# A hybrid decoder block on one core: both products of a bank ahead of their Squares in the linear attention, and one sum of the down projection queued behind the low part next to it

## The chip, the core and the metric

The kernel runs on one core of a Trainium2 chip. The metric is the device time of one execution in microseconds (us); the smaller the better. Five engines run side by side, each with its own in-order queue: TensorE (PE; its weight loads are shown apart as PEld), VectorE (DVE), ScalarE (ACT), GpSimd (POOL) and SyncE (SP, which issues most transfers here). They wait for one another through semaphores.

## The reference, cut to what matters

One decoder layer over 512 tokens of width 1024, in float32. A projection gives the inputs of two token mixers: a gated linear attention (4 heads, keys of 128, values of 256) and a sparse attention. Their outputs are merged, projected and added to the input; a SwiGLU channel mixer of width 2816 follows.

```
b = cumsum(log_a)                       # per head, in chunks of 64 tokens
qe, ke, kd = q*exp(b), k*exp(-b), k*exp(b_last - b)
o = causal(qe @ ke.T) @ v               # inside a chunk
o = o + qe @ s_prev                     # the state carried from the chunks before
o = o * rsqrt(mean(o*o) + eps) * norm_g # per token and head, over 256 values
...
f = (silu(h @ w_ffn_gate) * (h @ w_ffn_up)) @ w_ffn_down
x = x + rms_norm(f, norm_ffn_post)
```

The two places of the change are the line `o = ...` of the linear attention with the sum of squares of its norm, and the product with `w_ffn_down`.

## The kernel before, in words

**Products.** Float32 products are made in three passes: an operand is split into a high part (a cast, usually on ACT) and a low part (source minus high part, on DVE), and `three` (lines 266 to 276) issues high x high, high x low and low x high, seen in the trace as lines L269, L274 and L275. L274 loads the high part of the weight once more, and L275 loads its low part. `split` (L301 the cast, L303 the low part) makes the two parts. In a few products the low parts are left out and float32 operands go in as they are; such a matmul shows as two entries.

`restart()` makes the next 256-column product issue its second pass as two passes of 128 columns. It is called at chosen places; one is in the loop over the eight plain row blocks of the down projection.

**Linear attention.** Each head goes through `gla_prep`, `gla_attn`, `gla_state`, `gla_out` and `gla_end`; these steps are woven between the products of the input projection (`eproduct`, made in seven half-size products of a Strassen-like form). `gla_out(h)` is where the change is. It has four blocks of 128 tokens. Two PSUM banks (`ps`, tag `acc`) hold two blocks each, 256 columns per block. For a block n it issues the product of the masked scores with the values (L806), for n > 0 a second product of the query with the carried state (L808), and then an ACT `Square` of that block (L809) with the sum over the row in `ssq`. Heads 0 and 1 use plain float32 products; heads 2 and 3 use `three`, so that their products stand under L269, L274 and L275. When the four sums are there, `rsqrt_mean` makes the factor (L317 on DVE, L318 on POOL), ACT scales the four blocks (L817), and `gla_end` transposes them (L832).

**Down projection.** The first 8 row blocks of the weight are done plainly (`sd`). The rest is four units u of the same seven-product form. The list `seq` gives the order of the 28 products: for u = 0 and 1 in turn a11, s2, s3, s1, a22, s4, a12, so that u = 1 has the places j = 7 to 13, and s3, s1, a22, s4 of it are j = 9, 10, 11, 12. `make(j)` prepares the weight of product j: `dsum` makes its sum on DVE where there is one, `split` makes the high and low parts (`lows[j]` is the DVE instruction of the low part), and for some j `dload` starts a transfer of the next unit's quarter. `make(j + 3)` is called after product j. The sum s4 (L1915) is r12 minus s2; the quarter r12 of unit 1 lands in the second half of the buffer `c_two`, by a transfer that `make(6)` starts.

**What sets the order.** Tiles are allocated by name, and the program's planner orders the instructions of each engine by when it estimates their inputs to be ready, with program order as the priority; the waits between engines follow from the data. A PSUM bank is guarded as a whole: a product into one half of a bank waits for a read of the other half. `tc.issue_after(x)` fixes an order by hand: what is issued inside stands behind `x` in the queue of x's engine, without a wait for x to end. `dsum` takes such an `after`, which before the change is used for the sum s2 alone.

Of the kernel before, what the change touches and what calls it, by code (L numbers as in the profile page):

```python
# [11 lines left out]
AF = mybir.ActivationFunctionType  # L12
OP = mybir.AluOpType
# [161 lines left out]
def hybrid_block_kernel(ctx: ExitStack, tc: tile.TileContext, I, outT):  # L175
    nc = tc.nc
    act, dve, pool, pe = nc.scalar, nc.vector, nc.gpsimd, nc.tensor
# [13 lines left out]
    def bank(tag):  # L191
        return psum.tile([128, 512], F32, tag=tag, bufs=2, name="ps_" + tag)
# [47 lines left out]
    for key in with_gla + with_cmp + with_att + late:  # L240
        kind, n = key
# [23 lines left out]
    def three(o, w, x, start, stop):  # L265

        (wh, wl), (xh, xl) = w, x
        n = o.shape[1]
        pe.matmul(o, wh, xh, start=start, stop=False, skip_group_check=True)  # L269
        cut = [slice(0, 128), slice(128, 256)] if fresh[0] and n == 256 else [slice(0, n)]  # L270
        if n == 256:
            fresh[0] = False
        for c in cut:
            pe.matmul(o[:, c], wh, xl[:, c], start=False, stop=False, skip_group_check=True)  # L274
        stk["pe"] = pe.matmul(o, wl, xh, start=False, stop=stop, skip_group_check=True)  # L275
        return stk["pe"]
# [23 lines left out]
    def split(hi, lo, src, after=None):  # L300
        act.copy(hi, src)  # L301
        with tc.issue_after(after.ins) if after else nullcontext():
            return dve.tensor_tensor(out=lo, in0=src, in1=hi.bitcast(F32), op=OP.subtract)  # L303

    def token_sums(acc, tag, blocks=range(NT)):

        ps = bank(tag)
        for a in range(len(acc)):
            for i in blocks:
                stk["sums"] = pe.matmul(ps[:, i:i + 1], acc[a][:, i * 128:(i + 1) * 128], ones[:, 0:1],  # L310
                                        start=(a == 0 and i == blocks[0]), stop=(a == len(acc) - 1),
                                        skip_group_check=True)
        return ps

    def rsqrt_mean(out, ps, n, eps):
        with tc.high_priority():
            dve.tensor_scalar(out=out, in0=ps, scalar1=1.0 / n, scalar2=eps, op0=OP.mult, op1=OP.add)  # L317
            return pool.tensor_tensor(out=out, in0=out, in1=mhalf[:, 0:out.shape[1]], op=OP.pow)  # L318

    def over_partitions(rs, tag, blocks=range(NT), after=None):  # L320
        ps = bank(tag)
        with tc.issue_after(after.ins) if after else nullcontext():
            for i in blocks:
                stk["over"] = pe.transpose(ps[:, i * 128:(i + 1) * 128], rs[:, i:i + 1].to_broadcast([128, 128]),
                                           ident)
        return ps
# [260 lines left out]
    for g in range(3):  # L587
        pss = [bank(t) for t in tags[g]]
        for c in range(4):
# [6 lines left out]
            for i, kk, m in turns:  # L596
                if (g, c, i, kk, m) == (0, 3, 2, 0, 0):
                    ps = token_sums([acc_x], "acc")
# [4 lines left out]
                o = pss[i][:, 0:TW[g]]  # L603
                x, y = ((hu, wh), (hul, wh), (hu, wl))[m]
# [3 lines left out]
        if g == 0:  # L608
            ps = over_partitions(rs_x, "acc")
# [36 lines left out]
    lows = []  # L646
# [145 lines left out]
    def gla_out(h, after=None):  # L792
        q3, qk, ku, dec, kut, ss = gst[h]
        at = ats[h % 2]
        ps = [bank("acc"), bank("acc")]
        ssq = gt.tile([128, NT], F32, tag="gssq", bufs=2, name="gssq")
        o = gt.tile([128, NT, 256], F32, tag="go", bufs=1, name="go")
        for n in range(NT):
            out = ps[n // 2][:, (n % 2) * 256:(n % 2) * 256 + 256]
            if h >= 2:  # L800
                with tc.issue_after(after.ins) if after else nullcontext():
                    three(out, two_of[h, "a"][n], two_of[h, "v", n], True, n == 0)
                    if n > 0:
                        three(out, two_of[h, "q"][n], two_of[h, "s"][n - 1], False, True)
            else:
                pe.matmul(out, at[:, n, :], tok[n][:, h * 256:(h + 1) * 256], start=True, stop=(n == 0))  # L806
                if n > 0:
                    pe.matmul(out, q3[:, n].rearrange("p s t -> p (s t)"), ss[:, n - 1, :], start=False, stop=True)  # L808
            act.activation(out=o[:, n, :], in_=out, func=AF.Square, accum_out=ssq[:, n:n + 1])  # L809
        rs = gt.tile([128, NT], F32, tag="grs", bufs=2, name="grs")  # L810
        rsqrt_mean(rs, ssq, 256, EPS)

        def scaled(after=None):
            for n in range(NT):
                out = ps[n // 2][:, (n % 2) * 256:(n % 2) * 256 + 256]
                with tc.issue_after(after.ins) if after else nullcontext():
                    act.activation(out=o[:, n, :], in_=out, func=AF.Copy, scale=rs[:, n:n + 1])  # L817

        if h < 2:
            rest[h] = scaled  # L820
        else:
            scaled()
        gst[h] = o
# [97 lines left out]
    for h in range(2):  # L921
        steps.append(lambda h=h: gla_state(h))
        steps.append(lambda h=h: gla_out(h))
        steps.append(lambda h=h: [gla_attn(h + 1), rest.pop(h)(stk["cast"])])
        steps.append(lambda h=h: gla_prep(h + 2))
        steps.append(lambda h=h: gla_end(h))
# [429 lines left out]
    for n in range(8):  # L1356
        ps = bank("sc")
# [41 lines left out]
    def w_slot(which):  # L1399

        if which == "w":
            return (wts.tile([128, 1024], F32R, tag="whi", bufs=2, name="whi"),
                    wts.tile([128, 1024], F32R, tag="wlo", bufs=2, name="wlo"))
        if which in ("d0", "d1", "c"):
            t = double(which)
            return t[:, 0:1024], t[:, 1024:2048]
        tags = {"u": ("uu", "uu"), "g3": ("g3h", "g3l"), "rw": ("rw", "rw")}[which]
        return tuple(wtile(t) for t in tags)
# [20 lines left out]
    for n in range(3):  # L1429
        ps = bank("mm")  # L1430
# [454 lines left out]
    draw, dw, loaded, lows = {}, {}, {}, {}  # L1885
    two_raw = double("c", F32)

    def dload(u, q):
        if u >= 4:
            return  # L1890
        if u == 3:
            raw = flat(quad("hh%d" % ("12", "22", "21", "11").index(q), F32, "raw" + q))
        elif q == "12":
            raw = two_raw[:, 1024:2048]
        else:
            raw = wts.tile([128, 1024], F32, tag="wraw", bufs=3, name="wraw")
        r, c = int(q[0]) - 1, int(q[1]) - 1
        with tc.issue_after(loaded[1, "22"].ins) if u == 3 else nullcontext():
            loaded[u, q] = nc.sync.dma_start(raw[:, :KW], I["w_down"][2 * u + r, :, c * KW:(c + 1) * KW])
        draw[u, q] = raw[:, :KW]  # L1900

    def dsum(u, name, after=None):
        r11, r12, r21, r22 = [draw[u, q] for q in ("11", "12", "21", "22")]
        if name == "s2":
            dve.tensor_tensor(out=r21, in0=r11, in1=r21, op=OP.subtract)
            x = two_raw[:, :KW]
            with tc.issue_after(after.ins) if after else nullcontext():
                dve.tensor_tensor(out=x, in0=r22, in1=r21, op=OP.subtract)
            draw[u, "s3"], draw[u, "s2"] = r21, x
        elif name == "s1":  # L1910
            dve.tensor_tensor(out=r11, in0=r11, in1=draw[u, "s2"], op=OP.add)
            draw[u, "s1"] = r11
        elif name == "s4":
            x = draw[u, "s2"]
            dve.tensor_tensor(out=x, in0=r12, in1=x, op=OP.subtract)  # L1915
            draw[u, "s4"] = x


# [6 lines left out]
    ends = {}  # L1925

    def make(j):
        if j >= len(seq):
            return
        u, a, b = seq[j]  # L1930
        behind = ends.get(j - 5) or ends.get(j - 7) if a == "s2" else None
        with tc.issue_after(behind.ins) if behind else nullcontext():
            dsum(u, a, (None, lows.get(7), None, ends.get(j - 3))[u])
        hi, lo = [x[:, :KW] for x in w_slot(("w", "g3", "w")[j % 3])]
        lows[j] = split(hi, lo, draw[u, a if a[0] == "s" else a[1:]])
        dw[u, a] = (hi, lo)
        if a in after_form and u < 2:
            dload(u + 1, after_form[a])
# [3 lines left out]
    for n in range(8):  # L1942
        ps = bank(("mm", "sc", "acc", "tp")[n % 2 + n // 4 * 2])
# [13 lines left out]
        if n == 6:  # L1957
            for q in ("21", "11", "22", "12"):
                dload(0, q)
            make(0)  # L1960
            make(1)
    make(2)

    def last_forms(i):
# [141 lines left out]
    ps = bank("tp")  # L2106
# [32 lines left out]
    for k in range(4):  # L2139
        for i in range(2):  # L2140
            c, x = i * 128, byrow[:, i, k * 128:(k + 1) * 128]
# [4 lines left out]
    for k in range(2):  # L2146
        dve.scalar_tensor_tensor(out=y2[k][:, t], in0=back[:, k * 256:k * 256 + 256], scalar=g_fpost[:, k:k + 1],
                                 in1=x1s[k][:, t], op0=OP.mult, op1=OP.add)
# [87 lines left out]
```

## Time and profile before

| | |
|---|---|
| median of 3 runs | 829.97 us (829.06, 829.97, 830.84) |
| the profiled execution's own time | 828.92 us |
| its span, first to last instruction | 826.7 us |
| mean granted TensorE clock | 0.999 |
| PE busy | 817.1 us, 99% |
| PEld, DVE, ACT, POOL busy | 751.2, 638.8, 533.7, 138.8 us |

How to read it: the span is what the trace covers, and the profiled execution took 2.2 us more than that around it. Busy time counts a matmul from its start to its modelled end, so matmuls that overlap in the pipeline leave PE busy without a gap; how fast PE runs is read from the starts of its matmuls and from how many of them stand in a stretch. Times in the rows are microseconds from the start of the span; an entry in square brackets is the idle time of the engine before the instruction, and what ended it.

### The profile page before, as it was taken

The page shows a single profiled execution, that of the slowest core. Times are in us where ns is not written, and L with a number is a line of the kernel's source. Part 1 is how long each engine was busy: PE and PEld are TensorE (multiplying, and loading weights), DVE is VectorE, ACT ScalarE, POOL GpSimd, SP SyncE. Part 2 cuts the span into 40 slices and gives each one's busy share as a digit, 9 for nine tenths or more (in the row PEclk, how much of TensorE's full clock was granted, in tenths as well). Part 3 has the DMA queues.
Part 4 walks back from the last instruction along what each step waited for, and adds up shares of the span by engine and source line. Part 5 has one row for each costly group of instructions (what it writes and reads, how often), then busy time and mean ns, then how long its engine had stood idle before and what let it go on. Part 6 is the DMA issues. An engine that isn't in the chain of part 4 may idle for free.

```text
span 826.7 us, 15082 instructions
## 1 busy us (share of the span) xinstructions
PE 817.1 (99%) x5751; PEld 751.2 (91%) x5751; DVE 638.8 (77%) x1216; ACT 533.7 (65%) x988; POOL 138.8 (17%) x172
## 2 busy tenths in 40 slices
PE   9999999999999999999999999999999999999997
PEld 7898899899888787888888999999999999999997
DVE  7776898886377888877666479998888778929886
ACT  6647677775544989887645577866665566626453
POOL 0101122230030000010000364111221110001134
PEclk9999999999999999999999999999999999999999
DMA  8434466764152444454227758798888883235233
GB/s 275 126 107 118 119 120 125 165 142 114 52 185 50 109 122 105 102 119 112 69 72 262 234 157 232 178 235 204 182 184 202 198 192 90 77 94 173 97 102 103
DMA packets 44824, 117.87 MB, mean 143 GB/s; under 512 B 5868, under 2 KB 12028, under 8 KB 44624
## 3 DMA queue, kind: packets, MB, share of 16 engines
q1 hardware_dynamic: 31584, 82.71, 32.5%
q0 software_dynamic: 12464, 33.85, 22.5%
q8 instruction: 45, 0.74, 0.4%
q10 hardware_dynamic: 704, 0.36, 0.1%
q14 instruction: 27, 0.22, 0.1%
HBM read 102.21 MB, written 4.19 MB: 129 GB/s over the span
## 4 chain that ended last, share of the span: by engine, by line
PE 89%; DVE 4%; ACT 4%; DMA 1%; issue 1%; POOL 0%; POOLq 0%; ACTq 0%; DVEq 0%
PE ps_mm L269 13%; PE ps_mm L274 13%; PE ps_mm L275 13%; PE ps_sc L269 5%; PE ps_sc L275 5%; PE ps_sc L274 4%; PE ps_acc L269 3%; PE ps_acc L274 3%; PE ps_acc L275 3%; PE ps_tp L275 3%; PE ps_tp L274 3%; PE ps_tp L269 3%; PE ps_sc L605 2%; PE ps_tp L605 2%; PE ps_tp L1246 2%; PE ps_mm L605 1%
## 5 line engine op out<-in xcount | busy, mean ns | idle before, releaser
L269 PE MATMUL ps_mm<-hT_hi,whi 128*128 128x512 f32 (+1 forms) x268 | 98.4, 367 | 0.0
L275 PE MATMUL ps_mm<-hT_hi,wlo 128*128 128x512 f32 (+1 forms) x268 | 96.9, 362 | 0.0
L274 PE MATMUL ps_mm<-hT_lo,whi 128*128 128x512 f32 (+1 forms) x267 | 96.3, 361 | 0.0
L103 ACT CAST whi<-wraw 128x1024 fp32r<-128x1024 f32 (+2 forms) x61 | 59.0, 970 | 51.2 <-PE ps_mm L274 15.3
L110 DVE TENSOR_TENSOR wlo<-wraw,whi 128x1024 fp32r<-128x1024 f32 (+2 forms) x46 | 50.1, 1091 | 29.9 <-ACT whi L103 29.8
L269 PEld LDWEIGHTS ps_mm<-hT_hi,whi 128*128 128x128 f32 x268 | 50.4, 188 | 8.1
L275 PEld LDWEIGHTS ps_mm<-hT_hi,wlo 128*128 128x128 f32 x268 | 50.4, 188 | 8.1 <-DVE wlo L110 0.3
L274 PEld LDWEIGHTS ps_mm<-hT_lo,whi 128*128 128x128 f32 x267 | 50.2, 188 | 6.6
L1576 ACT CAST d_two<-s 128x1024 fp32r<-128x1024 f32 x26 | 27.2, 1045 | 35.9 <-PE ps_mm L275 18.7
L303 DVE TENSOR_TENSOR pl<-ps_tp,ph 128x512 fp32r<-128x512 f32 (+1 forms) x64 | 31.2, 490 | 13.0 <-ACT ph L301 12.0
L1583 DVE TENSOR_TENSOR d_two<-s,d_two 128x1024 fp32r<-128x1024 f32 x25 | 30.6, 1225 | 11.3 <-ACT d_two L1576 10.9
L1208 ACT ACTIVATE p<-p,mx 128x512 f32<-128x512 f32 (+3 forms) x64 | 35.7, 558 | 4.6 <-DVE mx L1206 4.1
L1206 DVE CUSTOM_DVE_ANT_0 p<-ps_sc,causal 128x512 f32<-128x512 f32 (+3 forms) x64 | 30.1, 487 | 9.7 <-PE ps_sc L1200 8.9
L107 POOL DMA_DIRECT2D wlo<-wraw x15 | 12.7, 849 | 147.4 <-ACT wlo L106 90.2
L1981 POOL TENSOR_TENSOR y<-y,us 128x256 f32<-128x256 f32 x12 | 13.5, 1143 | 98.5 <-DVE us L1977 98.5
L301 ACT CAST ph<-ps_tp 128x512 fp32r<-128x512 f32 (+1 forms) x64 | 26.5, 416 | 4.4 <-PE ps_tp L1246 3.4
L1246 PE MATMUL ps_tp<-ident,p 128*128 128x128 f32 x160 | 27.7, 272 | 0.0
L1246 PEld LDWEIGHTS ps_tp<-ident,p 128*128 128x128 f32 x160 | 20.8, 141 | 7.2 <-ACT pc L1130 0.4
L1576 ACT CAST c_two<-s 128x1024 fp32r<-128x1024 f32 x12 | 12.5, 1044 | 20.3 <-PE ps_acc L275 10.5
L1558 POOL DMA_DIRECT2D wlo<-in_w_gate x13 | 11.2, 858 | 80.4 <-ACT wlo L1556 71.9
L269 PE MATMUL ps_mm<-hT_hi,d_two 128*128 128x256 f32 x80 | 22.4, 279 | 0.0
L275 PE MATMUL ps_mm<-hT_hi,d_two 128*128 128x256 f32 x80 | 22.3, 279 | 0.0
(905 smaller groups left out, 3299.5 us busy)
## 6 DMA issues: line engine op xcount, KB each, us to landing
wraw<-in_w_t SPq DMA_DIRECT2D x36, 512.0 KB, 4.0
wraw<-in_w_gate SPq DMA_DIRECT2D x21, 512.0 KB, 4.4
rw<-in_w_up SPq DMA_DIRECT2D x19, 512.0 KB, 8.2
wlo<-wraw POOLq DMA_DIRECT2D x15, 512.0 KB, 4.5
wlo<-in_w_gate POOLq DMA_DIRECT2D x13, 512.0 KB, 7.7
w_uu<-in_w_up POOLq DMA_DIRECT2D x19, 256.0 KB, 8.7
wraw<-in_w_proj SPq DMA_DIRECT2D x8, 512.0 KB, 3.5
wraw<-in_w_out SPq DMA_DIRECT2D x8, 512.0 KB, 4.3
```

The lines of the kernel that those rows point to most:

```text
L103: self.cast = self.nc.scalar.copy(h, r)
L110: self.nc.vector.tensor_tensor(out=l, in0=r, in1=h.bitcast(F32), op=OP.subtract)
L269: pe.matmul(o, wh, xh, start=start, stop=False, skip_group_check=True)
L274: pe.matmul(o[:, c], wh, xl[:, c], start=False, stop=False, skip_group_check=True)
L275: stk["pe"] = pe.matmul(o, wl, xh, start=False, stop=stop, skip_group_check=True)
L303: return dve.tensor_tensor(out=lo, in0=src, in1=hi.bitcast(F32), op=OP.subtract)
L605: pe.matmul(o, x[:, k, t], y[:, w], start=(k == 0 and m == 0), stop=(k == KD - 1 and m == 2))
L1206: dve.tensor_tensor_reduce(out=o, in0=s, in1=causal[:, S - 128 * (i + 1):S], scale=-1.0, scalar=-NEG, op0=OP.add, op1=OP.min, accum_out=mx ...
L1208: act.activation(out=o, in_=o, func=AF.Exp, scale=-1.0, bias=mx[:, i:i + 1], accum_out=z[:, i:i + 1])
L1246: pe.transpose(tp[:, i * 128:(i + 1) * 128], p[:, OFF[i] + k * 128:OFF[i] + (k + 1) * 128] if i else p0, ident)
L1576: stk[names[0]] = act.copy(hi, t)
L1583: stk["lo"] = dve.tensor_tensor(out=lo, in0=t, in1=hi.bitcast(F32), op=OP.subtract)
```

## The change

In `gla_out` the Squares of blocks 0 and 1 are issued after the products of both blocks, and those of blocks 2 and 3 after the products of both; there are as many instructions as before. In `dsum` the sum s4 of unit 1 is queued behind the low part of the weight one place earlier (`lows[11]`, the low part of a22). `after` is handed over for s4 of every unit, but only unit 1 uses it. The argument for s2 is what it was.

```diff
             else:
                 pe.matmul(out, at[:, n, :], tok[n][:, h * 256:(h + 1) * 256], start=True, stop=(n == 0))
                 if n > 0:
                     pe.matmul(out, q3[:, n].rearrange("p s t -> p (s t)"), ss[:, n - 1, :], start=False, stop=True)
-            act.activation(out=o[:, n, :], in_=out, func=AF.Square, accum_out=ssq[:, n:n + 1])
+            for m in range(n - 1, n + 1) if n % 2 else ():
+                act.activation(out=o[:, m, :], in_=ps[n // 2][:, (m % 2) * 256:(m % 2) * 256 + 256], func=AF.Square,
+                               accum_out=ssq[:, m:m + 1])
...
         elif name == "s4":
             x = draw[u, "s2"]
-            dve.tensor_tensor(out=x, in0=r12, in1=x, op=OP.subtract)
+            with tc.issue_after(after.ins) if after and u == 1 else nullcontext():
+                dve.tensor_tensor(out=x, in0=r12, in1=x, op=OP.subtract)
             draw[u, "s4"] = x
...
         with tc.issue_after(behind.ins) if behind else nullcontext():
-            dsum(u, a, (None, lows.get(7), None, ends.get(j - 3))[u])
+            dsum(u, a, lows.get(j - 1) if a == "s4" else (None, lows.get(7), None, ends.get(j - 3))[u])
```

## The prediction, made before the result was known

> **What bounds the kernel now.** I read the page first: how busy each engine is, then the chain of work that ended last.
>
> ```profile
> span 826.7 us, 15082 instructions
> ...
> PE 817.1 (99%) x5751; PEld 751.2 (91%) x5751; DVE 638.8 (77%) x1216; ACT 533.7 (65%) x988; POOL 138.8 (17%) x172
> ...
> PE 89%; DVE 4%; ACT 4%; DMA 1%; issue 1%; POOL 0%; POOLq 0%; ACTq 0%; DVEq 0%
> ```
>
> PE sets the time: it is busy for 817.1 of 826.7 us, so a microsecond that PE loses in the middle has nowhere to be made up. The two stages that the change touches are next, by the view of windows (PE, PEld, DVE, ACT, POOL, each with its instructions).
>
> ```profile
> 128.00:198.00 70.00, 68.59 (x535) 65.86 (x534) 58.23 (x116) 50.19 (x111) 15.45 (x18) 1.00 0.64 145
> ...
> 751.00:800.00 49.00, 48.94 (x421) 48.74 (x421) 43.87 (x54) 22.18 (x31) 13.34 (x12) 1.00 0.45 146
> ```
>
> In the linear attention PE has 1.41 us without work; in the down projection it has 0.06 us, with DVE close behind (43.87 of 49 us). The view of waits says what PE and PEld waited for between 128 and 230 us, and, last row, between 745 and 800 us (total, times, longest).
>
> ```profile
> PEld ps_acc L806 <- ACT go L809: 1.8, 2, 1.5
> PEld ps_acc L269 <- ACT go L809: 0.7, 3, 0.3
> ...
> PEld ps_tp L832 <- ACT go L817: 0.2, 1, 0.2
> ...
> PEld ps_tp L275 <- DVE wlo L303: 0.3, 1, 0.3
> ```
>
> So PE waits five times for a Square (two waits in heads 0 and 1, three in heads 2 and 3), and once for a low part in down. These are the waits that the two edits can reach.
>
> **Part 1, the Squares.** It removes no instruction: 16 Squares and their products stay. What goes is the wait of a block's product for the Square of the other block in its bank. The dearest case is head 1, in the timeline of PE and of ACT:
>
> ```profile
> 161.62 0.59 PE L808 MATMUL ps_acc<-gs,gq 128*128 128x256 f32 x2
> 163.35 0.70 PE L806 MATMUL ps_acc<-tok,at 128*128 128x256 f32 x2 [1.14 <-ACT go L809]
> 163.89 0.59 PE L808 MATMUL ps_acc<-gs,gq 128*128 128x256 f32 x2
> 164.32 0.59 PE L806 MATMUL ps_acc<-tok,at 128*128 128x256 f32 x2
> ...
> 161.79 0.62 ACT L452 CAST whi<-wraw 128x512 fp32r<-128x512 f32 x1 [2.00 <-PE ps_acc L806]
> 162.31 0.62 ACT L455 ACTIVATE wlo<-wraw 128x512 fp32r<-128x512 f32 x1
> 162.84 0.36 ACT L809 ACTIVATE go<-ps_acc 128x256 f32<-128x256 f32 x1
> ```
>
> Blocks 0 and 2 are done, and blocks 1 and 3 stand behind a Square, which stands behind two 128x512 casts for another weight in ACT's queue. From 161.62 to 163.35 are 1.73 us for two passes that take 0.43 (163.89 to 164.32): 1.30 lost. The product after the wait lasts 0.70 instead of 0.59, 0.11 more. Head 1: 1.41 us. The row names no other releaser. Head 0 and a sample of head 3:
>
> ```profile
> 134.17 0.28 PE L269 MATMUL ps_mm<-et2gh,whi 128*128 128x256 f32 x1
> 134.52 0.70 PE L806 MATMUL ps_acc<-tok,at 128*128 128x256 f32 x2
> ...
> 219.31 0.28 PE L274 MATMUL ps_acc<-gsgl,gqe 128*128 128x256 f32 x1
> 219.57 0.38 PE L269 MATMUL ps_acc<-tok,gah 128*128 128x256 f32 x1
> 219.80 0.28 PE L274 MATMUL ps_acc<-tok,gah 128*128 128x256 f32 x1
> ```
>
> Head 0: a step of 0.35 where passes of this kind step by 0.12, and 0.70 for 0.59: 0.34 us. Heads 2 and 3: 0.26 and 0.23 for two steps of 0.12, so 0.25 lost, three times (the row of 0.7 in three waits): 0.75 us. Sum of part 1: 0.34 + 1.41 + 0.75 = **2.50 us**. The transposes' wait of 0.2 (L832 on L817) may go as well, since the last products and so the last Squares come earlier; it is not counted, and is in the range.
>
> What it adds is no wait on PE: the next user of these banks is the next head, far behind. On ACT the four Squares move later against their first product and earlier against the last, so the norm factor comes no later. What is moved: in head 0 the planner filled the wait with a product of the projection; now all seven products of the head can stand together, 14 passes of 0.215 = 3.0 us, and the passes that stood between its first two blocks (from the first row below to the second, 1.4 us) go behind them, up to 2 us later.
>
> ```profile
> 129.18 0.39 PE L269 MATMUL ps_mm<-hT_hi,feq 128*128 128x256 f32 x1
> ...
> 130.56 0.30 PEld L806 LDWEIGHTS ps_acc<-tok,at 128*128 128x128 f32 x2
> ```
>
> Their reader is an ACT copy and DVE sums, then weights needed several products on. Hidden as long as those are that far ahead; if not, one late operand costs what a wait cost above, 0.25 to 1.41 us. So part 1 lies between 2.7 us gained (the transposes' wait too) and nothing gained, and I take 2.50, since every term is a measured wait on the engine that sets the time.
>
> **Part 2, the sum s4 of unit 1.** DVE, then PE, in the timeline:
>
> ```profile
> 765.38 0.41 DVE L1977 TENSOR_TENSOR y<-ps_sc,y 128x256 f32<-128x256 f32 x1
> 766.81 1.09 DVE L1915 TENSOR_TENSOR c_two<-c_two 128x896 f32<-128x896 f32 x1 [1.01 <-DMA c_two<-in_w_down]
> 767.82 1.09 DVE L303 TENSOR_TENSOR wlo<-wraw,whi 128x896 fp32r<-128x896 f32 x1
> 768.82 1.08 DVE L303 TENSOR_TENSOR w_g3l<-wraw,w_g3h 128x896 fp32r<-128x896 f32 x1
> ...
> 770.15 1.08 DVE L303 TENSOR_TENSOR wlo<-wraw,whi 128x896 fp32r<-128x896 f32 x1
> ...
> 768.51 0.28 PE L269 MATMUL ps_tp<-dt3e,whi 128*128 128x256 f32 x1
> 768.62 0.28 PE L274 MATMUL ps_tp<-dt3hl,whi 128*128 128x256 f32 x1
> 768.96 0.39 PE L275 MATMUL ps_tp<-dt3e,wlo 128*128 128x256 f32 x1
> 769.18 0.28 PE L269 MATMUL ps_tp<-dt3e,whi 128*128 128x256 f32 x1
> ```
>
> s4 sits first in DVE's queue, 1.01 us idle on its transfer, and three low parts (j = 9, 10, 11) wait behind it though they don't need it. The first ends at 768.91, and PE needs it at 768.73. Behind the third, s4 leaves the first low part to start at 765.8: it ends at 766.9, 1.8 us early. The stall's own price: 0.34 for 0.11 and 0.22 for 0.12: 0.33 us. The larger price is the pace after it:
>
> ```profile
> 709.80:768.62 58.82, 58.82 (x522) 1.00 0.36 114
> 769.30:808.28 38.98, 38.98 (x333) 1.00 0.33 102
> ...
> 140.95:148.40 7.45, 7.45 (x68) 1.00 0.60 130
> ...
> 165.43:170.70 5.27, 5.27 (x47) 1.00 0.24 44
> ```
>
> Two or three matmuls of each count had begun before the window. So up to the stall PE starts a 256-column matmul every 58.82 / 519 = 113.3 ns, and right after it every 38.98 / 331 = 117.8 ns, at a granted clock of 1.00 in both. The earlier stretches show the same two paces (7.45 / 66 = 113, 5.27 / 45 = 117), the slow one right after head 1's wait. I read it as a state that a late operand can set and that lasts to the next break in the stream. Without the stall those 331 matmuls at the first pace take 331 x 4.5 ns = 1.49 us less. Part 2: 0.33 + 1.49 = **1.82 us**; bounds 0 (a stall elsewhere) and 1.82.
>
> The Trainium skill, page "TensorE: Matmul & The Clock Gate", section "Back-to-back issue gap", gives a warm gap of N / 2.4 + 2.5 ns, that is 109 ns for 256 columns, and knows no second pace. By that rule no stall slows what follows, the term of 1.49 falls away, and the sum would be 2.50 + 0.33 = 2.83 us; the windows of this trace, 113.3 and 117.8 ns at one clock, do not agree with a single gap.
>
> What s4's later place costs: the third low part ends at 771.2 in its row, and no later without the stall, so s4 ends by 772.3 instead of 767.9; its cast and low part follow.
>
> ```profile
> 771.38 0.95 ACT L301 CAST whi<-c_two 128x896 fp32r<-128x896 f32 x1 [1.80 <-PE ps_tp L274]
> ...
> 772.36 1.33 DVE L303 TENSOR_TENSOR wlo<-c_two,whi 128x896 fp32r<-128x896 f32 x1 [0.43 <-ACT whi L301]
> ...
> 776.48 0.28 PE L275 MATMUL ps_tp<-hT_hi,wlo 128*128 128x256 f32 x1
> ```
>
> The cast waits for PE to free its buffer until 771.38 anyway, so s4 delays it by 0.9 us at most, and the low part (it ended at 773.7) ends by 774.6. PE reads it at 776.48, or near 775.9 at the faster pace: 1.3 us to spare. Nothing waits on s4 but that cast. SP's next loads hang on the low part of j = 9, now earlier.
>
> **Sum.** 2.50 + 1.82 = 4.32 us off the profiled execution's 828.92 (826.7 of span and 2.2 around it): 824.6. That execution lies 1.05 below the median of the runs; the same 4.32 off 829.97 gives **825.6 us**.
>
> **Rivals.** (a) The pace is not the stall's doing: it belongs to the later products, or another late operand sets it again soon after. Then part 2 gives 0.33: 829.97 - 2.50 - 0.33 = 827.1. For: DVE is busy 90% in this stage. Against: unit 0's same products run at 113.3 ns inside the first window.
>
> (b) Part 1 is given back: the moved passes make later weights late, or head 1's gain meets the next late form. Only part 2 stays: 828.1. For: DVE is busy 58.23 of 70 us there. Against: ACT's rows show casts waiting for PE, not the reverse.
>
> (c) Neither edit shows: the planner's other choices bring equal waits back, 830.0. Against: the waits have a data cause that the edits remove.
>
> (d) Slower: an operand is a little late inside the long stretch of the feed-forward units, and sets the slow pace there.
>
> ```profile
> 555.70:708.00 152.30, 152.30 (x1346) 1.00 0.76 178
> ```
>
> These 1344 matmuls run at 113.3 ns; at 117.8 they take 6.0 us more, which with both gains is 829.97 - 4.32 + 6.0 = 831.7. It decides from the point where more than 4.32 / 0.0045 = 960 of them are slow. For: one wait of 0.3 did it at 768.62. Against: neither edit touches an operand of that stage, and a restart stands ahead of it.
>
> **How the numbers follow.** The forecast (825.6) has 0.56, (a) 0.16, (b) 0.14, (c) 0.06, (d) 0.08. About 0.2%, 1.66 us, is what a measurement of this kernel tells from no change. Faster by more than that, under 828.3: the forecast, (a) and half of (b), 0.79. Within it: the other half of (b) and (c), 0.13. Slower: (d), 0.08. The low end has both parts, the transposes' 0.2 and the early slow stretches turned fast (some 210 matmuls, 0.9 us), with 0.6 for the runs' scatter: 823.9. The high end is (b) with 0.8 of scatter and of early fast stretches turned slow: 828.9.
>
> **What would show it.** Part 1 is right if no wait of PE or PEld on L809 is left, and the seven products of a head stand together. Part 2 is right if DVE has no wait on the transfer ahead of L1915, PE has no gap near 766 us, and the windows after it show 113 ns. I am wrong if PE's idle time turns up elsewhere between 128 and 226 us, or if the pace there or after 555 us has changed.

## The result and the profile after

The kernel after takes **825.08 us** (median of six runs, 824.08 to 825.67) beside 829.43 of the kernel before: a ratio of 0.9948, 95% interval 0.9934 to 0.9963. A second measurement on another occasion gave 825.18 beside 828.20, ratio 0.9963 (0.9951 to 0.9976). The prediction said 825.6 in a range of 823.9 to 828.9. The profiled execution of after took 825.66 us, with a span of 823.4.

Line numbers of the changed kernel stand two higher behind the Squares (three behind s4): a Square is L810, s4 is L1918. The page of the kernel after, span and busy time of PE, PEld, DVE, ACT and POOL, and the chain by engine:

```profile
span 823.4 us, 15085 instructions
...
PE 813.9 (99%) x5751; PEld 748.9 (91%) x5751; DVE 639.1 (78%) x1216; ACT 534.3 (65%) x988; POOL 138.7 (17%) x172
...
PE 87%; DVE 4%; ACT 4%; DMA 2%; issue 2%; POOL 1%; SPq 0%; DVEq 0%; ACTq 0%; POOLq 0%
```

PE has as many matmuls as before and is busy for 3.2 us less. It still sets the time. The view of windows of after, with the same columns as before:

```profile
128.00:198.00 70.00, 69.91 (x549) 67.50 (x548) 59.13 (x118) 51.03 (x112) 15.46 (x18) 1.00 0.64 145
...
707.92:804.71 96.79, 96.79 (x856) 96.79 (x855) 74.59 (x98) 48.77 (x72) 16.06 (x15) 1.00 0.35 110
751.00:800.00 49.00, 49.00 (x435) 49.00 (x434) 43.39 (x54) 23.37 (x32) 13.67 (x13) 1.00 0.49 157
```

In the linear attention PE is without work for 0.09 us where it was for 1.41, and does 14 more matmuls in the same 70 us. In down it does 435 where it did 421, and the whole stretch has one pace: 96.79 / 854 = 113.3 ns a matmul (two had begun before the window), with no stall and no slow part behind one. The waits of PEld of after between 128 and 230 us, where five waits for a Square and one of the transposes stood:

```profile
PEld ps_mm L269 <- DVE kstw L524: 0.3, 1, 0.3
PEld ps_mm L269 <- DVE sr L524: 0.2, 1, 0.2
```

Neither was touched by the change. Head 1 in the timeline of PE, and DVE in down, both of after:

```profile
161.32 1.02 PE L806 MATMUL ps_acc<-tok,at 128*128 128x256 f32 x4
162.18 0.59 PE L808 MATMUL ps_acc<-gs,gq 128*128 128x256 f32 x2
162.61 0.59 PE L806 MATMUL ps_acc<-tok,at 128*128 128x256 f32 x2
...
163.91 0.59 PE L808 MATMUL ps_acc<-gs,gq 128*128 128x256 f32 x2
```

```profile
763.99 1.08 DVE L303 TENSOR_TENSOR wlo<-wraw,whi 128x896 fp32r<-128x896 f32 x1
765.61 1.09 DVE L303 TENSOR_TENSOR w_g3l<-wraw,w_g3h 128x896 fp32r<-128x896 f32 x1 [0.54 <-ACT w_g3h L301]
767.01 0.42 DVE L1980 TENSOR_TENSOR us<-ps_acc,us 128x256 f32<-128x256 f32 x1 [0.32 <-PE ps_acc L275]
767.86 1.35 DVE L303 TENSOR_TENSOR wlo<-wraw,whi 128x896 fp32r<-128x896 f32 x1 [0.42 <-ACT whi L301]
769.13 1.08 DVE L1918 TENSOR_TENSOR c_two<-c_two 128x896 f32<-128x896 f32 x1
```

The products of head 1 follow each other every 0.43 us, none waits. In down the low part of j = 9 is done at 765.07, 1.8 us before PE loads it, and s4 starts without a wait on its transfer. On one pair of traces the forecast looks confirmed step by step. The runs below show that two of its largest terms are not there in every execution.

### The profile page after: what moved, and what is told of

Read it like the earlier page. It is cut to its first block, busy times and chain, and to the rows that moved or that the text cites. A ratio compares the mean times of both kernels' runs of the same rounds, so it can differ in the third digit from the quotient of the medians.

```text
span 823.4 us, 15085 instructions
## 1 busy us (share of the span) xinstructions
PE 813.9 (99%) x5751; PEld 748.9 (91%) x5751; DVE 639.1 (78%) x1216; ACT 534.3 (65%) x988; POOL 138.7 (17%) x172
## 4 chain that ended last, share of the span: by engine, by line
PE 87%; DVE 4%; ACT 4%; DMA 2%; issue 2%; POOL 1%; SPq 0%; DVEq 0%; ACTq 0%; POOLq 0%
PE ps_mm L269 13%; PE ps_mm L275 13%; PE ps_mm L274 13%; PE ps_sc L275 4%; PE ps_sc L269 4%; PE ps_sc L274 4%; PE ps_acc L275 4%; PE ps_acc L269 4%; PE ps_acc L274 4%; PE ps_tp L275 3%; PE ps_tp L274 3%; PE ps_tp L269 3%; PE ps_tp L605 2%; PE ps_tp L1248 2%; PE ps_sc L605 1%
```

## Experiments

In the tables of this section two stretches are worked out from the starts of PE's matmuls in each trace, counted from 0: from the 750th to the 1500th (linear attention, all four heads) and from the 5000th to the 5750th (down). The first is the place of part 1, the second of part 2. The column head 1 is the time from the first to the last entry of L806 and L808 there.

**Part 1 alone.**

```diff
-            act.activation(out=o[:, n, :], in_=out, func=AF.Square, accum_out=ssq[:, n:n + 1])
+            for m in range(n - 1, n + 1) if n % 2 else ():
+                act.activation(out=o[:, m, :], in_=ps[n // 2][:, (m % 2) * 256:(m % 2) * 256 + 256], func=AF.Square,
+                               accum_out=ssq[:, m:m + 1])
```

> The kernel before with part 1 alone; the sum s4 stays at its old place. My theory: 2.5 us under the kernel before (head 0 0.34, head 1 1.41, heads 2 and 3 0.75), no wait of PE on a Square, while the wait on the low part in down (0.3 us near 766 us) and the pace of 117.8 ns behind it stay. Rival b (part 1 is given back): within 0.5 us of the kernel before, with new waits between 128 and 226 us.

Measured: 826.12 us beside 828.78 of before, ratio 0.9964 (0.9950 to 0.9978), so 2.7 us less; rival b falls. But down did not do what I expected: the slow pace is there, and it doesn't begin at s4's stall. Part 1 alone, windows, a Square's surroundings on ACT, and the fourth product of head 1 (where before waits) and the stalled product of down on PE:

```profile
707.56:749.95 42.39, 42.39 (x376) 42.39 (x375) 26.24 (x37) 22.23 (x37) 0.00 (x0) 1.00 0.24 71
750.11:806.53 56.42, 56.42 (x482) 56.42 (x480) 49.77 (x62) 26.83 (x36) 15.83 (x16) 1.00 0.41 136
```

```profile
161.90 0.62 ACT L452 CAST whi<-wraw 128x512 fp32r<-128x512 f32 x1 [2.04 <-DMA wraw<-in_w_t]
162.42 0.63 ACT L455 ACTIVATE wlo<-wraw 128x512 fp32r<-128x512 f32 x1
162.96 0.36 ACT L810 ACTIVATE go<-ps_acc 128x256 f32<-128x256 f32 x1
...
162.07 0.59 PE L806 MATMUL ps_acc<-tok,at 128*128 128x256 f32 x2
...
749.95 0.33 PE L275 MATMUL ps_mm<-dt3e,wlo 128*128 128x256 f32 x1
750.11 0.28 PE L269 MATMUL ps_mm<-dt3e,whi 128*128 128x256 f32 x1
```

At 749.95 us a low part of the second product of down (j = 1) is late by so little that no wait is listed: the step is 0.16 us instead of 0.11. Behind it PE goes from 113.3 ns (42.39 / 374) to 117.8 (56.42 / 479) to the end of down. On ACT the two casts ahead of head 1's Squares stand behind a **transfer**, for which the first of them waits 2.04 us, and the first Square starts only at 162.96. PE has started the fourth product at 162.07, so nothing is lost. This is what part 1 does: it takes the late transfer out of PE's way.

**Part 2 alone, four traces.**

```diff
-                dve.tensor_tensor(out=x, in0=r12, in1=x, op=OP.subtract)
+            with tc.issue_after(after.ins) if after and u == 1 else nullcontext():
+                dve.tensor_tensor(out=x, in0=r12, in1=x, op=OP.subtract)
...
-            dsum(u, a, (None, lows.get(7), None, ends.get(j - 3))[u])
+            dsum(u, a, lows.get(j - 1) if a == "s4" else (None, lows.get(7), None, ends.get(j - 3))[u])
```

> The kernel before with part 2 alone; the Squares stay one behind each product. My theory: 1.8 us under the kernel before (0.33 of the wait and 1.49 of the pace of 331 matmuls), the waits on the Squares stay, and the matmuls after 769 us start every 113.3 ns. Rival a (the pace is not the stall's doing): 0.33 us under the kernel before, with 117.8 ns after 769 us.

Measured: 828.39 us beside 828.78, ratio 0.9995 (0.9984 to 1.0006). A gain of 1.8 us in every execution (0.9978) is outside the interval; rival a's 0.33 (0.9996) and no gain at all are inside it. The trace, though, is as I expected in down (113.3 ns throughout), and its execution was the fastest of twelve (827.22; up to 830.69). So executions of one kernel differ by more than the terms in question, and the trace says where: head 1 had no wait. The first cast and the fourth product of head 1 in that trace:

```profile
160.87 0.63 ACT L452 CAST whi<-wraw 128x512 fp32r<-128x512 f32 x1
...
162.95 0.59 PE L806 MATMUL ps_acc<-tok,at 128*128 128x256 f32 x2
```

The transfer had landed in time, the casts ran 0.8 us before the head's first product, and the Squares came behind them without delay. The order on ACT is that of before. From here on my theory was that both large terms hang on transfers whose landing differs between executions. Three more traces of part 2 alone and one more of the kernel before were taken to test it.

> The kernel before, unchanged, for a second trace of it. After the first three runs my theory is changed: two of the waits that I counted hang on transfers whose landing differs between executions. Head 1's 1.41 us is there where the transfer for ACT's cast ahead of the Squares lands after about 161.5 us on this trace's scale (it landed in time in the trace of part 2 alone, and PE waited for no Square in head 1), and the wait and the slow pace in down are there where the transfer for s4, or an earlier low part, is late. So this second trace shows each of the two either as in the first or not at all, and the time is lower by 1.4 us for head 1 and by 1.8 us for down where it is not. Rival, the waits belong to the order of the work: both are as in the first trace.

> Part 2 alone once more, for a second trace of it. Its first trace had neither head 1's wait nor a slow pace in down, and was the fastest of its 12 executions (827.2 us; the others lie near 827.6, 829.1 and 830.4). My theory: a slower execution has head 1's wait (1.4 us), or a slow pace in down that begins at a low part near 752 us (some 480 matmuls, 2.1 us) as in the trace of part 1 alone, or both. Rival: no wait and no slow pace in down, and the time is lost elsewhere.

> Part 2 alone, for a third trace. Its 12 timed executions lay between 827.2 and 830.7 us and its two traces so far (827.2 and 827.0) are of fast ones. My theory: an execution over 828.5 us shows head 1's wait for a Square behind a late transfer (up to 1.4 us), or a slow pace in down set by a low part near 750 us (2.1 us), or both; one under 828 shows neither. Rival: the time of a slower one is lost outside the two stages, which part 2 alone and part 1 would share.

> The same, for a fourth trace: over 828.5 us with head 1's wait or a slow pace in down, or under 828 us with neither. Rival: neither is there in a slower execution.

All traces of the two kernels with the old Squares, and for comparison those with the new ones (us):

| kernel | its execution | head 1 | 750th to 1500th | 5000th to 5750th |
|---|---|---|---|---|
| before | 828.92 | 4.21 | 111.40 | 87.32 |
| before, second trace | 827.68 | 3.44 | 110.90 | 86.06 |
| part 2 alone | 827.22 | 2.80 | 110.28 | 85.90 |
| part 2 alone, second | 826.97 | 2.81 | 110.37 | 85.86 |
| part 2 alone, third | 828.02 | 4.08 | 111.57 | 85.89 |
| part 2 alone, fourth | 830.16 | 3.82 | 111.35 | 88.01 |
| part 1 alone | 827.11 | 2.80 | 108.38 | 87.67 |
| after | 825.66 | 2.80 | 108.43 | 85.87 |
| after, second trace | 825.09 | 2.80 | 108.36 | 85.89 |

**Head 1.** The second trace of before, the third and the fourth of part 2 alone, the cast ahead of the Squares:

```profile
161.99 0.62 ACT L452 CAST whi<-wraw 128x512 fp32r<-128x512 f32 x1 [1.19 <-DMA wraw<-in_w_t]
```

```profile
162.45 0.62 ACT L452 CAST whi<-wraw 128x512 fp32r<-128x512 f32 x1 [1.86 <-DMA wraw<-in_w_t]
```

```profile
162.32 0.62 ACT L452 CAST whi<-wraw 128x512 fp32r<-128x512 f32 x1 [1.57 <-PE ps_acc L806]
```

Head 1's first product starts at 161.72, 161.55 and 161.68 in them. Set against that start, the cast comes 0.27, 0.90 and 0.64 us later, and head 1 loses 0.64, 1.28 and 1.02 us against 2.80. In the first trace of before it is 1.03 later and 1.41 lost. The loss is the lateness plus 0.37 or 0.38 in all four; in the two traces where the cast came 0.8 and 0.9 us ahead of the product, nothing is lost. The wait is set by the landing of the transfer. In the last of these rows and in the first trace of before the releaser named is "PE ps_acc L806"; in four other traces with a late cast it is the transfer. The view of transfers settles it. The same transfer in the first trace of before, the fourth of part 2 alone and the first of part 2 alone (last column: us from issue to landing):

```profile
wraw<-in_w_t SPq DMA_DIRECT2D x1, 512.0 KB, 6.3
```

```profile
wraw<-in_w_t SPq DMA_DIRECT2D x1, 512.0 KB, 5.8
```

```profile
wraw<-in_w_t SPq DMA_DIRECT2D x1, 512.0 KB, 4.4
```

SP issues it at 155.44, 156.46 and 156.44, so it lands at 161.71, 162.25 and 160.79, and the cast starts 0.07 to 0.08 us behind the landing in these as in all other traces. The two waits named for PE are waits for the transfer.

**Down.** The second trace of before has s4 at its old place and no stall. DVE and the window:

```profile
766.35 1.09 DVE L1915 TENSOR_TENSOR c_two<-c_two 128x896 f32<-128x896 f32 x1 [0.59 <-DMA c_two<-in_w_down]
```

```profile
709.74:805.96 96.22, 96.22 (x851) 96.22 (x850) 73.94 (x97) 48.61 (x71) 16.40 (x14) 1.00 0.34 111
```

s4 waited 0.59 us instead of 1.01, the low part behind it came in time, and the pace is 113.3 ns (96.22 / 849) to the end: 86.06 us, 0.2 more than with s4 behind. Part 2 was worth 0.2 us in this execution. The fourth trace of part 2 alone is the opposite, late without s4's doing:

```profile
744.35 1.09 DVE L1908 TENSOR_TENSOR c_two<-wraw 128x896 f32<-128x896 f32 x1 [4.91 <-DMA wraw<-in_w_down]
...
757.12 0.41 DVE L1978 TENSOR_TENSOR us<-ps_mm,us 128x256 f32<-128x256 f32 x1
```

```profile
753.20:757.51 4.31, 4.31 (x40) 4.31 (x39) 4.31 (x8) 1.22 (x2) 1.22 (x1) 1.00 0.71 187
757.87:809.58 51.71, 51.71 (x441) 51.71 (x440) 44.83 (x55) 25.04 (x34) 14.34 (x15) 1.00 0.40 131
```

A transfer for the first sums of down landed late; DVE ran behind; PE stalled at 752.55 and again at 757.51, where the next product's bank was read by DVE until 757.53; and behind the second stall it ran at 117.8 ns (51.71 / 439); behind the first it had run at 113.3. Counted from the 5000th matmul, that first sum starts after 10.16 us in this trace and after 9.78 in that of part 1 alone, the two that turned slow between 750 and 758 us; in the eight other traces of before, after, part 2 alone and the one with a restart it starts after 9.0 to 9.6, and none of them stalls there.

So the four executions of part 2 alone have what the changed theory said: 826.97 and 827.22 neither loss, 828.02 head 1 (it lies between the two marks that I had set, 828 and 828.5), 830.16 both.

**The stall stays, a restart behind it.** Both parts undone.

```diff
     for j, (u, a, b) in enumerate(seq):
+        if j == 10:
+            restart()
         end = down_product(j)
```

> The kernel before, both parts undone, with the kernel's own restart (the next 256-column passes cut into two of 128) ahead of the product of down that follows the stalled one. The stall stays. My theory, that the stall sets a state which the next restart ends: the stall of 0.33 us is still there, the some 20 matmuls up to the restart start every 117.8 ns and the some 310 behind it every 113.3 ns, and the time is 310 x 4.5 ns = 1.40 less 0.13 for the restart, so about 1.25 us under the kernel before. Rival a, that the slow pace belongs to these products: 117.8 ns behind the restart too, and 0.13 us over the kernel before.

The trace gives the cleanest reading of the pace, by windows ahead of the stall, behind it, and behind the restart:

```profile
710.88:769.93 59.05, 59.05 (x523) 59.05 (x522) 41.79 (x57) 30.23 (x47) 3.76 (x3) 1.00 0.36 113
770.08:772.20 2.12, 2.12 (x20) 2.12 (x19) 2.06 (x3) 0.71 (x1) 0.98 (x1) 1.00 0.67 184
773.14:807.93 34.79, 34.79 (x309) 34.79 (x308) 30.56 (x38) 17.00 (x25) 10.46 (x11) 1.00 0.28 96
```

113.3 ns (59.05 / 521), 117.8 (2.12 / 18), 113.3 (34.79 / 307), all at a granted clock of 1.00. The slow pace does not belong to the products, and a split pass ends it. In this execution the stall itself was 0.04 us (a step of 0.15 instead of 0.11). The median, 828.47 us beside 828.78 (ratio 0.9998, 0.9987 to 1.0009), shows none of the 1.25 us that I expected. By the traces that is no contradiction, since the slow pace is not in every execution and the restart costs 0.13 in each; the interval cannot tell it from a small gain.

**A low part made late.** The kernel after, the low part of j = 9 computed two or three times more, with the same values.

```diff
-        lows[j] = split(hi, lo, draw[u, a if a[0] == "s" else a[1:]])
+        src = draw[u, a if a[0] == "s" else a[1:]]
+        lows[j] = split(hi, lo, src)
+        for _ in range(2 if j == 9 else 0):
+            with tc.issue_after(lows[j].ins):
+                lows[j] = dve.tensor_tensor(out=lo, in0=src, in1=hi.bitcast(F32), op=OP.subtract)
```

> The kernel after, with the low part that stalled before (j = 9 in down) computed three times instead of once, the same values, so that it ends 2.0 us later, at about 767.1 us where PE wants it at 766.9. My theory: a stall of 0.2 to 0.3 us at that product, and behind it the pace of 117.8 ns for some 331 matmuls: 1.8 us over the kernel after. Rival a: the stall alone, 0.3 us over it, with 113.3 ns behind.

> The same with the low part computed four times, 3.0 us later: late by about 1.2 us, with the low parts of the next two products late by less. My theory: 1.2 us of stall and 117.8 ns behind the last of the stalls, 2.7 us over the kernel after. Rival a: 1.2 us over it, with 113.3 ns behind. If the pace depends on how long the stall is, this run and the one with the short stall differ in it.

With two more, the stalled product on PE and the windows:

```profile
765.59 0.35 PE L275 MATMUL ps_tp<-dt3e,wlo 128*128 128x256 f32 x1
765.77 0.28 PE L269 MATMUL ps_tp<-dt3e,whi 128*128 128x256 f32 x1
```

```profile
706.54:765.59 59.05, 59.05 (x524) 59.05 (x522) 42.83 (x58) 30.33 (x47) 3.76 (x3) 1.00 0.35 113
765.77:804.87 39.10, 39.10 (x333) 39.10 (x333) 34.51 (x43) 18.67 (x26) 13.71 (x13) 1.00 0.32 102
```

A stall of 0.07 us (a step of 0.18) and then 332 steps of 117.8 ns: 1.5 us lost to the pace for 0.07 of waiting. The execution took 825.45 us, only some 0.3 over the medians of after, but it was 1.1 us ahead of the first trace of after at the 250th matmul, so I compare the stretch. From the 5000th to the 5750th matmul it takes 87.04 us against 85.87, so 1.2 us in all; 0.3 comes back in the tail, where after has a wait on POOL that the late kernel hasn't. In this one trace a late low part set the slow pace, as my theory had it, less that 0.3 of size. With three more, the planner moved the product, and PE waited twice:

```profile
767.78 0.38 PE L275 MATMUL ps_tp<-dt1e,w_g3l 128*128 128x256 f32 x1 [1.51 <-DVE w_g3l L303]
768.00 0.29 PE L269 MATMUL ps_tp<-dt1e,w_g3h 128*128 128x256 f32 x1
...
768.58 0.28 PE L275 MATMUL ps_tp<-dt1e,w_g3l 128*128 128x256 f32 x1
768.78 0.39 PE L275 MATMUL ps_tp<-dt3e,wlo 128*128 128x256 f32 x1
...
769.24:805.62 36.38, 36.38 (x324) 36.38 (x322) 31.94 (x40) 17.41 (x24) 12.81 (x12) 1.00 0.32 107
```

Here I was wrong: behind two real gaps the pace is 113.3 ns (36.38 / 321). The stretch takes 88.24 us, 2.4 more than in after: 2.0 in the two gaps and 0.4 in the wait on POOL in the tail, which is longer here. A long wait need not set the slow pace.

**After again, and two variants of it.**

> The kernel after, unchanged, for a second measure beside the kernel before and for the base of the two other runs. My theory as changed by the traces: part 1 gives 1.9 us in every execution and up to 1.4 more where the transfer ahead of head 1's Squares lands late; part 2 gives 0.2 us where nothing is late in down and 1.5 to 1.7 where the slow pace is set. So between 2.1 and 5.0 us in one execution, and about 3.5 us under the median of the kernel before. Rival, the first figures hold in every execution: 4.3 us.

825.18 us beside 828.20, 3.0 us less (ratio 0.9963, 0.9951 to 0.9976): nearer to the changed theory's 3.5 than to 4.3, though the first measurement's 4.35 with its own interval allows both. Over all measurements the kernel before ran 44 times with a median of 828.5 us (standard deviation 1.1), and the instructions of after 18 times, those of the next variant among them, with 825.2 (0.7): 3.3 us less, and a narrower scatter.

```diff
-            for m in range(n - 1, n + 1) if n % 2 else ():
-                act.activation(out=o[:, m, :], in_=ps[n // 2][:, (m % 2) * 256:(m % 2) * 256 + 256], func=AF.Square,
+            for m in range(NT) if n == NT - 1 else ():
+                act.activation(out=o[:, m, :], in_=ps[m // 2][:, (m % 2) * 256:(m % 2) * 256 + 256], func=AF.Square,
```

> The kernel after with all four Squares of a head behind all of its products. PE waits for no Square in either kernel. My theory: the first two Squares of a head go 0.7 us later on ACT, so the norm factor and the scaled blocks too; in the trace of after the scaled blocks of head 3 end 0.1 us before the transposes that read them, and those of head 2 0.6 us before, so the transposes wait some 0.6 and 0.1 us, and the time is 0.7 us over the kernel after. Rival, only the products' wait for a Square counts, and the Squares have room: within 0.2 us of the kernel after.

825.08 us (ratio 0.9968, 0.9957 to 0.9980), the same as after. The planner put every instruction of every engine where it stands in after, so this tests nothing about late Squares; it is a third measurement of after. How much room the Squares have was not found out.

```diff
         def one(i):
+            if u == 1 and i == 0:
+                restart()
             eproduct(u, i)
...
+    restart()
     ffn_half(0, w0, first, range(6, 8))
...
+    restart()
     ffn_both(range(1, 4))
...
     w2 = st.next(("g", 2))
+    restart()
...
     for j, (u, a, b) in enumerate(seq):
+        if j == 2:
+            restart()
         end = down_product(j)
```

with the split of a restart allowed for 512-column passes too.

> The kernel after with restarts (one pass cut into two halves, 0.13 us each) at five more places: ahead of the second unit pair of the linear attention's projections, at three places of the feed-forward part between 475 and 520 us, and at the third product of down. My theory, that the slow pace is a state which a restart ends: some 130 matmuls at 99 us and some 200 at 478 to 520 us turn from 117.8 to 113.3 ns (0.6 and 0.9 us), less 0.6 for the five restarts, so 0.5 to 0.9 us under the kernel after, and fewer slow executions. Rival, the slow pace belongs to the products there: 117.8 ns behind the restarts too, and 0.6 us over the kernel after.

824.91 us (ratio 0.9960, 0.9947 to 0.9974), 0.3 under the 825.18 of after in the same measurement, which their scatter does not tell from nothing. Windows of after, then of the kernel with restarts:

```profile
99.17:114.59 15.42, 15.42 (x132) 15.42 (x131) 13.71 (x26) 10.54 (x22) 3.46 (x4) 1.00 0.57 127
498.52:506.77 8.25, 8.25 (x72) 8.25 (x71) 8.21 (x16) 4.29 (x9) 4.13 (x5) 1.00 1.03 309
```

```profile
98.85:107.69 8.84, 8.84 (x80) 8.84 (x79) 7.56 (x16) 6.39 (x14) 1.73 (x2) 1.00 0.49 119
498.00:505.20 7.20, 7.20 (x65) 7.20 (x65) 7.17 (x15) 3.49 (x8) 3.33 (x5) 1.00 1.04 329
```

Between these two traces the pace turned at both places from 117.8 ns (15.42 / 131, 8.25 / 70) to 113.3 (8.84 / 78) and to 113 (7.20 us with some 64 steps). Counted from 90 to 128 and from 470 to 525 us, 454 steps are slow in this trace of after, 326 in its second and 201 in the one with restarts: 1.1 or 0.6 us less at 4.5 ns a step, and five restarts cost 0.65. A step of 0.17 us set the slow pace again at 110.7 us, and 64 steps near 480 us stayed slow. But the turn at 99 us is not shown to be the restart's doing: in 7 of the 13 other traces, the second of after among them, these products begin at 113.3 ns without one. At 498 us 12 of the 13 others are slow. The two paces are the same in another stage; that the restarts make this kernel faster is not shown.

## Why the prediction was right, and where it was not

The time was right, 825.6 against 825.08 and 825.18, but that it came so near was in part luck: over all executions before has a median of 828.5 us, 1.5 below the 829.97 that I subtracted from, and the gain is 3.3, 1.0 below the 4.32 that I subtracted; the two errors mostly cancel. Both edits take away the waits that I named. The sizes of the terms came from one execution, and two of them were read as fixed.

**Part 1, 2.50 us.** Measured: 2.66 us between the medians of part 1 alone and before; between traces, 108.3 to 108.4 us from the 750th to the 1500th matmul in all with the new Squares, and 110.3 to 111.7 in all with the old, so 1.9 to 3.3 us, 2.7 on average. By its steps:
- Head 0, 0.34: from the first product of head 0 to that of head 1 it is 31.92 us in the first trace of before, 32.2 to 32.3 in the six others with the old Squares, and 31.5 with the new. So 0.5 in the execution that I read, 0.8 in the rest: undersized. What the rest is made of was not followed further.
- Heads 2 and 3, 0.75, and the transposes' 0.2 that I left out: from the last product of head 1 to the 1500th matmul it is 73.8 to 74.0 us with the old Squares and 72.7 with the new, 1.1 to 1.2. The 0.2 belonged in the sum; it is gone in every trace with the new Squares. Some 0.2 more is not accounted for.
- Head 1, 1.41: **this step failed.** I wrote "The row names no other releaser", and against rival (b), "ACT's rows show casts waiting for PE, not the reverse". The casts waited for a transfer, and the loss is 0, 0.01, 0.64, 1.02, 1.26, 1.28 or 1.41 us in the seven traces with the old Squares, 0.8 on average. The sign to look for another was in the row: after 2.00 us of idle time the cast reads and writes the weight alone (whi<-wraw), not the bank of its named releaser.

**Part 2, 1.82 us.** Between the two first traces: 808.28 - 804.71 = 3.57 us at the end of down, less the 1.88 by which after was ahead at its start, is 1.69; 0.3 of it is lost again in the tail to a wait on POOL, and 1.45 is left at the 5750th matmul. For that pair the working held, 0.33 for the stall and 4.5 ns a matmul behind it. **What failed is the step from that execution to the median**: s4's transfer sets the stall in two of the three traces with s4 at its old place that weren't slow already, and in the second trace of before part 2 is worth 0.2. The mean over the traces with the old s4 (87.32, 86.06 and 87.67; the one with the restart left out) is 87.0, and over those of after and of part 2 alone 86.2 (85.87, 85.89, 85.90, 85.86, 85.89, 88.01): some 0.8 us, from few traces; the medians of part 2 alone and before differ by 0.4 and do not tell it from nothing. The bounds, 0 to 1.82, held it; the value taken was at their upper end. Nor does a late operand always set the slow pace, as the term of 1.49 took for granted (last section).

So part 1 gave slightly more than 2.50 (head 0 and the transposes up, head 1 down) and part 2 less than 1.82: 2.7 and 0.8 make 3.5, between the two measured differences of 4.35 and 3.02.

**The start.** The profiled execution of before was 0.4 to 1.0 us ahead of 11 of the 13 others at its 250th matmul, 54.67 us against 55.06 to 55.68. The two profiled executions differ by 3.26: 2.97 in the linear attention and 1.45 in down, less 1.02 at the start and 0.14 elsewhere. That I scaled the forecast to the median of the runs covered this by luck; I had not looked whether the start scatters.

**The cost of s4's later place**, which I put at nothing with 1.3 us to spare, is nothing: it ends at 770.21, before the 772.3 that I allowed, and its low part ends by 772.4.

**The range.** Its low end counted 0.9 us for early slow stretches turned fast. In the linear attention the pace is worth much less: from head 1's last product to the 1500th matmul the second trace of before has 68 slow steps and the second of part 2 alone 164, and they take 73.81 and 73.89 us. Where PE ran faster, more of its time went into steps of over 0.13 us (1.90 us of them above the usual step, against 1.64).

**The rivals.** (a) was right that an operand other than s4 can set the slow pace: it did so near 750 us in two traces of other variants, in none of after. That the pace belongs to the products is refuted by the restart. (b) and (c) fell by part 1 alone. (d) did not come: from 560 to 698 us all 14 traces run at 113.3 ns. The 2.83 us by a single gap came from a formula that the section cited there does not give for such a stream (last section).

**What was to show it**: no wait on a Square, no wait on the transfer ahead of s4, no gap near 766 us and 113 ns behind came as written. The seven products of head 0 don't all stand together: its first block is still 1.8 us ahead of the rest, which costs nothing.

## What to carry to other kernels

Where a wait stands behind a transfer, one trace gives its size in one execution; take two or three traces of the kernel before, and look at the idle time ahead of each instruction that the waiting engine depends on, before the wait goes into a sum at its full size. An edit that takes a late transfer out of the bounding engine's way is worth the mean of what that transfer costs, and a narrower scatter. Where an engine is busy 99% of the time, count its instructions per microsecond by stretch: the pace can change at a full clock, without a wait in any list.

## What the runs showed of the hardware

At a granted clock of 1.00, pairs of a 128x128 weight load and a 256-column matmul ran at two steady paces, **113.3 and 117.8 ns** a pair, for hundreds of matmuls each. Passes of 128 columns, as the restart makes them, were followed by the fast one every time: 89 such passes stand in the 14 traces, the steps behind each are back at 113 to 114 ns within ten matmuls, and ten of them stand straight behind the slow pace (nine between 534 and 539 us, one in the kernel with the restart in down).

What sets the slow pace stays open. In down, four weight loads that were late by some 0.04 to 0.07 us (steps of 0.15, 0.16, 0.17 and 0.18 us instead of 0.11) were followed by it, and of four full gaps (0.20, 0.34, 0.43 and 1.78 us from one matmul to the next) only the one of 0.34 was. So a load that was hardly late cost 1.5 us there, and one that was 1.5 us late nothing beyond its wait. But this is no rule of short and long: at other places of the same traces, one and the same delay was followed by either pace. Behind a step of 0.35 us near 79 us four traces run at 117.8 ns and ten at 113.3; here the first trace of before and the first of part 2 alone, 44 steps each:

```profile
79.62:84.62 5.00, 5.00 (x45) 5.00 (x45) 3.27 (x6) 4.99 (x6) 0.00 (x0) 1.00 0.47 147
```

```profile
80.48:85.67 5.19, 5.19 (x46) 5.19 (x46) 3.46 (x7) 5.18 (x6) 0.00 (x0) 1.00 0.41 147
```

Behind a step of 0.17 or 0.18 us near 108 us four traces are slow and four fast, behind one of 0.15 or 0.16 between 531 and 536 us nine and five. Near 156 us a step of 0.17 even ended the slow pace in four of six traces. A delay can turn the pace either way, and its length does not tell which.

The Trainium skill, page "TensorE: Matmul & The Clock Gate", section "Back-to-back issue gap", gives N / 2.4 + 2.5 ns as the warm gap of an isolated matmul, by estimate 109 ns for 256 columns. It says that in a stream of weight loads and matmuls both set the spacing. In the trace no long stretch of such pairs runs at 109 ns; all traces show the two paces.

The second thing is how much a transfer's landing differs between executions of nearly the same program: the transfer ahead of head 1's cast landed 4.3 to 6.3 us after its issue, so the cast started between 0.9 us ahead of the head's first product and 1.1 us behind it, and the first sum of down between 9.0 and 10.2 us behind the 5000th matmul, in traces of kernels that issue these transfers alike.
